# A kernel that plans its own order: new lengths for TensorE's and VectorE's pieces in the plan

## The chip, the cores and the metric

The kernel runs on one NeuronCore of a Trainium2 chip, in one launch. The metric is the device time of that launch in microseconds, the median of the runs shown. A core has five engines that matter here, each with its own instruction stream: TensorE (PE, with PEld for its weight loads), VectorE (DVE), ScalarE (ACT), GpSimd (POOL) and SyncE (SP), which only issues DMAs.

## The reference

It is one layer of a hybrid decoder trunk in float32. A prompt of 1024 tokens and 8 single tokens of a sample group share the weights, so that the kernel works on 1032 columns. D is 1024, there are 4 heads of 256 over 256 memory tokens, and the hidden width of the last part is 2816.

```python
def layer(x, pool_hist, conv_hist, start_pos, mk, mv, g_mix, w_in, pool_map_w, pool_map_b, pool_scale,
          conv_dw_w, conv_dw_b, conv_ln_g, conv_ln_b, w_out, g_attn, w_q, w_o, g_ffn, w_gate, w_up, w_down):
    h = rmsnorm(x, g_mix)
    u = h @ w_in
    a = u[..., :POOL_WIDTH]
    val = u[..., POOL_WIDTH:POOL_WIDTH + CONV_CH]
    gate = u[..., POOL_WIDTH + CONV_CH:]
    glu = val * jax.nn.sigmoid(gate)
    a_ext = jnp.concatenate([pool_hist, a], axis=1)
    g_ext = jnp.concatenate([conv_hist, glu], axis=1)
    ya = pool_mixer(a_ext, start_pos, pool_map_w, pool_map_b, pool_scale)
    yb = conv_mixer(g_ext, conv_dw_w, conv_dw_b, conv_ln_g, conv_ln_b)
    x = x + jnp.concatenate([ya, yb], axis=-1) @ w_out
    x = x + cross_attn(rmsnorm(x, g_attn), mk, mv, w_q, w_o)
    h = rmsnorm(x, g_ffn)
    x = x + (jax.nn.silu(h @ w_gate) * (h @ w_up)) @ w_down
    return x, a_ext[:, -POOL_HIST:], g_ext[:, -CONV_HIST:]
```

`pool_mixer` subtracts each channel from its mean over a trailing window of 2, 4, 8 or 16 tokens and applies a 128x128 map to each group. `conv_mixer` is a depthwise convolution of width 31, a layer norm and a swish. `cross_attn` takes keys and values of the memory, which `mem_kv` makes with `w_k` and `w_v` and which are outputs too. A last rmsnorm gives `y`.

## The kernel before

Activations lie with channels on the 128 partitions and tokens along the free axis. Float32 products are made of three passes of a rounded type: every operand is split into a high half (a rounded copy) and a low half (what the copy lost), and `PASSES` multiplies high by high, high by low and low by high. So each weight tile and each activation tile needs two pieces of work before TensorE may read it: the high half on ACT or POOL (`split`, L346 or L348), the low half on DVE or POOL (L357). For some weights the low half is an accumulating DMA from POOL's queue instead (`split_by_dma`, L368 to L375).

The stages follow each other: input projection with convolution and pooling (matmuls of 344 columns, L457); keys and values of the memory (L827, 256 columns, and L901, 512 columns); the pool map `pmap` and the two output projections `oa` and `ob`; queries, scores and values of the attention; its output projection `po`; then the gated feed-forward part. That part is written as a block product with seven instead of eight multiplications a 2x2 block (`product`, L1290, 258 columns a matmul): VectorE adds each product's bank into its sums (`plus_sums`, L1305), ScalarE copies some of them (`copy_sums`, L1309), and either VectorE or GpSimd does the products and sums between SBUF tiles (L1331, L1313). The up and gate half runs over 22 tiles f, the down half over 16 units u of four chunks, and a last plain part (`fd`, L1587) over what is left of the hidden width.

PSUM holds two wide buffers (`mm`) and two of one bank (`ms`). Every third `product` takes the two `ms` banks, `pr_0` and `pr_1`, and the others an `mm` buffer. A new product can only start in a buffer when its last reader is through.

What sets the order: the kernel body does not issue instructions. It records pieces with `add`: which engines may do the piece, and for each a length in microseconds, the function that emits it, and what it reads and writes. `Program.order` then plays the pieces against each other as a list scheduler. It holds a time at which each engine is free, starts at each step the piece that can start first (within a slack of 0.02 to 0.3 us the one recorded earlier), gives a piece that several engines may do to the one that ends it first, assigns buffers, and keeps VectorE's pieces with two SBUF inputs (`lock=True`) out of GpSimd's. The instructions are issued in that order on each engine. So a length in the plan costs nothing on the chip, but moves pieces in an engine's queue and from one engine to another.

In the plan a VectorE piece is a fixed part and 1.05 ns a column. The fixed part is 0.065 us up to the attention's output projection and 0.148 from there on:

```python
    fixed = {"DVE": 0.065}
    def dve(n):
        return fixed["DVE"] + 0.00105 * n
```

A TensorE piece has a number written out at each place: 0.146 a matmul of 344 columns, 0.109 of 256, 0.217 of 512, 0.1195 of 258 in `product`, 0.1097 of 258 in the last part.

## Time and profile before

| | |
|---|---|
| median of 3 runs | 1264.19 us (1262.49 to 1268.23) |
| the profiled execution's own time | 1266.04 us |
| its span | 1264.2 us |
| PE, DVE, ACT, POOL busy, share of the span | 96%, 72%, 42%, 39% |
| granted TensorE clock, mean | 0.991 |

The page of the profile gives busy time by engine, the span in 40 slices with the granted clock of TensorE, and groups of instructions. Further views are asked of the trace: who waited for whom, the instructions in order of time (start, duration, engine, line, operation, the idle time before it and what ended that), and the busy time of each engine in chosen stretches. A matmul row's duration is its time in the pipeline, so the rate of matmuls is read from a stretch and its count.

### The profile page before, as it was taken

How to read it: one execution, taken by the hardware profiler on the slowest of the kernel's cores; microseconds unless marked ns; L12 is line 12 of the kernel's file. 1: busy time of each engine (PE TensorE's matmuls, PEld its weight loads, DVE VectorE, ACT ScalarE, POOL GpSimd, SP SyncE). 2: the span in 40 equal slices, each digit the busy share in tenths (PEclk: the TensorE clock that was granted, in tenths of full speed). 3: DMA queues.
4: the chain of work that ended last, by engine and by line, in shares of the span. 5: the costliest groups of instructions: out<-in, count | busy, mean ns of one | idle time of the engine just before them, and what ended most of it. 6: DMA issues, size and time to landing. Idle time of an engine off the chain costs nothing.

```text
span 1264.2 us, 22138 instructions
## 1 busy us (share of the span) xinstructions
PE 1218.6 (96%) x8958; PEld 1196.0 (95%) x8958; DVE 909.9 (72%) x1542; ACT 531.8 (42%) x733; POOL 497.8 (39%) x436
## 2 busy tenths in 40 slices
PE   8999997999999999999999999999999999999996
PEld 7999986999999889989999999999999989999996
DVE  7899888667367786578776868686766767766644
ACT  6766658454233443453222222222222355533544
POOL 3578741032101112125353334334433558768401
PEclk9999997999999999999999999999999999999998
DMA  7447696644265663231333133313313598889703
GB/s 278 104 83 167 144 248 171 204 106 158 89 220 198 233 259 143 85 118 59 110 101 108 61 119 109 109 60 109 118 68 118 207 297 231 215 209 246 173 23 113
DMA packets 60453, 188.62 MB, mean 149 GB/s; under 512 B 8064, under 2 KB 11840, under 8 KB 59072
## 3 DMA queue, kind: packets, MB, share of 16 engines
q1 hardware_dynamic: 52288, 157.74, 35.3%
q0 software_dynamic: 8064, 29.47, 13.1%
q8 instruction: 70, 1.15, 0.4%
q14 instruction: 31, 0.25, 0.1%
HBM read 153.55 MB, written 33.64 MB: 148 GB/s over the span
## 4 chain that ended last, share of the span: by engine, by line
PE 73%; DVE 8%; issue 7%; DMA 6%; ACT 3%; POOL 2%; SPq 0%; DVEq 0%; POOLq 0%; ACTq 0%
PE pr L1290 41%; PE ps L457 12%; PE fd L1587 5%; PE oa L457 4%; PE ob L457 4%; DVE cacc L663 2%; DMA dr<-in_w_dn 2%; PE sc L1000 2%; PE pv L1058 2%; DMA raw<-in_w_v 2%; DVE su L1331 1%; DMA hb<-hb 1%; POOL w L357 1%; ACT hb L368 1%; PE psg L457 1%
## 5 line engine op out<-in xcount | busy, mean ns | idle before, releaser
L1305 DVE TENSOR_TENSOR su<-pr,su 128x258 f32<-128x258 f32 (+1 forms) x204 | 109.5, 558 | 98.2 <-PE pr L1290 91.6
L1290 PE MATMUL pr<-ab,wG 128*128 128x258 f32 x1056 | 134.8, 284 | 6.1 <-DVE su L1305 3.8
L1290 PEld LDWEIGHTS pr<-ab,wG 128*128 128x128 f32 x1056 | 129.9, 189 | 7.8 <-DVE su L1305 4.4
L1290 PE MATMUL pr<-ab,wTa 128*128 128x258 f32 x1056 | 134.1, 283 | 0.0
L1290 PE MATMUL pr<-ab,wTb 128*128 128x258 f32 x1056 | 130.5, 283 | 0.0
L1290 PEld LDWEIGHTS pr<-ab,wTa 128*128 128x128 f32 x1056 | 130.0, 189 | 0.0
L1290 PEld LDWEIGHTS pr<-ab,wTb 128*128 128x128 f32 x1056 | 128.5, 189 | 0.0
L457 PE MATMUL ps<-xop,w 128*128 128x344 f32 x720 | 114.1, 320 | 0.6 <-DMA w<-in_w_in 0.6
L457 PEld LDWEIGHTS ps<-xop,w 128*128 128x128 f32 x720 | 113.3, 188 | 0.9 <-DMA w<-in_w_in 0.9
L1290 PE MATMUL pr<-hb,dV 128*128 128x258 f32 x768 | 99.5, 286 | 3.1 <-ACT x L1309 2.1
L1290 PEld LDWEIGHTS pr<-hb,dV 128*128 128x128 f32 x768 | 96.0, 192 | 3.9 <-ACT x L1309 2.4
L457 PE MATMUL ps<-xq,w 128*128 128x344 f32 x576 | 94.8, 321 | 0.0
L457 PE MATMUL po<-oo,w 128*128 128x344 f32 x576 | 91.0, 320 | 0.4 <-DVE oo L1063 0.4
L457 PEld LDWEIGHTS po<-oo,w 128*128 128x128 f32 x576 | 90.7, 188 | 0.7 <-DVE oo L1063 0.7
L457 PEld LDWEIGHTS ps<-xq,w 128*128 128x128 f32 x576 | 90.6, 188 | 0.1
L1305 DVE TENSOR_TENSOR x<-pr,x 128x258 f32<-128x258 f32 (+1 forms) x122 | 63.7, 556 | 28.8 <-PE pr L1290 25.7
L1290 PE MATMUL pr<-hb,dW 128*128 128x258 f32 x576 | 75.6, 284 | 3.9 <-DMA hb<-hb 2.5
L663 DVE SCALAR_TENSOR_TENSOR cacc<-glu,vec,cacc 128x511 f32<-128x511 f32 (+14 forms) x116 | 77.0, 741 | 0.0
L1290 PEld LDWEIGHTS pr<-hb,dW 128*128 128x128 f32 x576 | 71.7, 189 | 5.1 <-DMA hb<-hb 3.2
L1331 DVE TENSOR_TENSOR su<-su,Rf 128x516 f32<-128x516 f32 x66 | 64.6, 981 | 10.8 <-ACT su L1338 10.4
L1587 PE MATMUL fd<-ho,w 128*128 128x258 f32 x576 | 70.0, 283 | 0.0
L1587 PEld LDWEIGHTS fd<-ho,w 128*128 128x128 f32 x576 | 69.4, 189 | 0.1
(319 smaller groups left out, 2330.2 us busy)
## 6 DMA issues: line engine op xcount, KB each, us to landing
gr<-in_w_gu SPq DMA_DIRECT2D x44, 512.0 KB, 3.4
hs<-hb SPq DMA_DIRECT2D x28, 516.0 KB, 6.9
hb<-hb POOLq DMA_DIRECT2D x21, 516.0 KB, 9.2
hb<-su SPq DMA_DIRECT2D x8, 1032.0 KB, 4.5
dr<-in_w_dn SPq DMA_DIRECT2D x16, 512.0 KB, 8.8
spcache_k<-in_cache_k SPq DMA_DIRECT2D x12, 512.0 KB, 4.7
raw<-in_w_in SPq DMA_DIRECT2D x10, 512.0 KB, 5.3
w<-in_w_in POOLq DMA_DIRECT2D x9, 512.0 KB, 6.8
```

What stands on the lines that cost most here:

```text
L357: e.tensor_tensor(dst(1), src(), f32(dst(0)), ALU.subtract)
L368: e.activation(dst(p), src, AF.Copy, scale=factor)
L457: e.matmul(ps[:, c, :CW], w[:, wi, cols], x[:, xi, c * CW : (c + 1) * CW], start=first and p == 0, stop=last and p == 2)
L663: e.scalar_tensor_tensor(acc[h][:, n:], src[:, : HALF - n], w, acc[h][:, n:], ALU.mult, ALU.add)
L1000: e.matmul(bank()[:, i * NMEM : (i + 1) * NMEM], qop[2 * h + dt][:, qi, tt * P : (tt + 1) * P], kk[:, ki, 2 * (h % 2) + dt], start=(dt == ...
L1058: e.matmul(ps[:, c], v[:, vi, m, col : col + P], pT[h][m][:, pi, sl], start=(m == 0 and p == 0), stop=(m == 1 and p == 2))
L1290: e.matmul(bank(c), w[:, wi, cols(j)], xs[0](j, xi)[:, c * TQ : (c + 1) * TQ], start=j == 0 and p == 0, stop=j == nj - 1 and p == 2)
L1305: from_sums(sums, "DVE", dve, lambda e, src, sl: e.tensor_tensor(as_banks(o(sl), src), src, as_banks(a(sl), src), ALU.add), [akey], [okey])
L1331: add({"Pool": pool_tt(TH), "DVE": dve(TH)}, lambda e: e.tensor_tensor(o(), o(), b(), ALU.mult), r + [(su[f], q)], [(su[f], q)], lock=True)
L1587: e.matmul(view(i), w[:, wi, col : col + P], hops[k][:, xi, lo + i * width // count : lo + (i + 1) * width // count], start=(k == 0 and p ...
```

## The change

The plan gets one function for TensorE's matmuls, 6 ns and 0.44 ns a column, in place of the numbers written out, and VectorE keeps the fixed part of 0.065 us to the end. By that function a matmul of 344 columns becomes 0.157 (was 0.146), of 256 columns 0.119 (0.109), of 512 columns 0.231 (0.217), of 258 columns in `product` 0.1195 as before and in the last part 0.1195 (0.1097). No instruction is added, removed or resized but for the pieces that go to another engine: counted over the whole order, 113 pieces go from GpSimd to VectorE, 90 from VectorE to GpSimd, 27 from GpSimd to ScalarE and 22 from ScalarE to GpSimd. Lines from 288 to 1512 stand one lower in the new file.

```diff
--- before.py
+++ after.py
@@ -280,13 +280,14 @@
         return ap.rearrange("p (c n) -> p c n", c=NCH)
 
 
+    def pe(n, count=1):
+        return (0.006 + 0.00044 * n) * count
+
     def act(n, ps=False, ptrs=0):
         return (0.05 if ps else 0.093) + 0.000833 * n + 0.093 * ptrs
 
-    fixed = {"DVE": 0.065}
-
     def dve(n):
-        return fixed["DVE"] + 0.00105 * n
+        return 0.065 + 0.00105 * n
 
     def pool_tt(n):
         return 0.09 + 0.00216 * n
@@ -457,7 +458,7 @@
                     e.matmul(ps[:, c, :CW], w[:, wi, cols], x[:, xi, c * CW : (c + 1) * CW],
                              start=first and p == 0, stop=last and p == 2)
 
-        add({"PE": 0.146 * 3 * len(spans)}, emit, list(wkeys) + (keys or [(x, 0), (x, 1)]),
+        add({"PE": pe(CW, 3 * len(spans))}, emit, list(wkeys) + (keys or [(x, 0), (x, 1)]),
             [(ps, c) for c in spans])
 
     def all3(ps):
@@ -826,7 +827,7 @@
                     for p, (wi, xi) in enumerate(PASSES):
                         e.matmul(ps[:, 0, i * NMEM : (i + 1) * NMEM], w[:, wi, block_cols(k)], memg[k // 4][:, xi, k % 4],
                                  start=(k == 0 and p == 0), stop=(k == KT - 1 and p == 2))
-                add({"PE": 0.327}, emit, wkeys + [(memg[k // 4], p, k % 4) for p in range(2)], [(ps,)])
+                add({"PE": pe(NMEM, 3)}, emit, wkeys + [(memg[k // 4], p, k % 4) for p in range(2)], [(ps,)])
         kf = scr(f"kf{q}", (P, 2, NMEM))
         add({"DVE": dve(512)}, lambda e: e.tensor_tensor(
             kf[:], ps[:, 0].rearrange("p (i m) -> p i m", i=2), Rm().unsqueeze(1).to_broadcast([P, 2, NMEM]), ALU.mult),
@@ -900,7 +901,7 @@
                         for m in range(2):
                             e.matmul(ps[:, m], memg[k // 4][:, xi, k % 4, m * P : (m + 1) * P], w[:, wi, col : col + 512],
                                      start=(k == 0 and p == 0), stop=(k == KT - 1 and p == 2))
-                add({"PE": 1.3}, emit, wkeys + [(memg[k // 4], p, k % 4) for p in range(2)], [(ps,)])
+                add({"PE": pe(512, 6)}, emit, wkeys + [(memg[k // 4], p, k % 4) for p in range(2)], [(ps,)])
         vf = scr(f"vf{c}", (P, 2, 512))
         for m in range(2):
             add({"ACT": act(512, True, 1)}, lambda e, m=m: e.activation(
@@ -1001,7 +1002,7 @@
                                  kk[:, ki, 2 * (h % 2) + dt], start=(dt == 0 and p == 0), stop=(dt == 1 and p == 2))
 
         o = 2 * (h % 2)
-        add({"PE": 1.31}, emit, [(qop[2 * h + dt], p) for dt in range(2) for p in range(2)] + [(kk, p, o) for p in range(2)], [pk])
+        add({"PE": pe(NMEM, 12)}, emit, [(qop[2 * h + dt], p) for dt in range(2) for p in range(2)] + [(kk, p, o) for p in range(2)], [pk])
         st = buf(f"sm{h}_{i2}", "sm", (P, 8))
 
         def top(e):
@@ -1058,7 +1059,7 @@
                         e.matmul(ps[:, c], v[:, vi, m, col : col + P], pT[h][m][:, pi, sl],
                                  start=(m == 0 and p == 0), stop=(m == 1 and p == 2))
 
-            add({"PE": 1.3}, emit, [(v, 0), (v, 1)] + [(pT[h][m], p, c) for p in range(2) for m in range(2)], [(ps, c)])
+            add({"PE": pe(512, 6)}, emit, [(v, 0), (v, 1)] + [(pT[h][m], p, c) for p in range(2) for m in range(2)], [(ps, c)])
             add({"ACT": act(512, True)}, lambda e, c=c, sl=sl: e.activation(oo[:, 0, sl], ps[:, c], AF.Copy), [(ps, c)], [(oo, 0, c)])
             add({"DVE": dve(512)}, lambda e, c=c, sl=sl: e.tensor_tensor(oo[:, 1, sl], ps[:, c], f32(oo[:, 0, sl]), ALU.subtract),
                 [(ps, c), (oo, 0, c)], [(oo, 1, c)])
@@ -1292,7 +1293,7 @@
 
         for n in range(0, nj, nj // steps):
             js = range(n, n + nj // steps)
-            add({"PE": 0.1195 * 6 * len(js)}, lambda e, js=js: emit(e, js),
+            add({"PE": pe(TQ, 6 * len(js))}, lambda e, js=js: emit(e, js),
                 [(w, 0), (w, 1)] + [k for j in js for k in xs[1][j]], [k for _, _, k in sums])
         return sums
 
@@ -1509,7 +1510,6 @@
         hops.append(ho)
 
 
-    fixed["DVE"] = 0.148
     for n in O_ORDER:
         proj_o(n)
         j, i = n % 4, n // 4
@@ -1588,7 +1588,7 @@
                                  start=(k == 0 and p == 0), stop=(k == 5 and p == 2))
 
         for w, keys, ks in ((wa, ka, range(4)), (wb, kb, (4, 5))):
-            add({"PE": 0.000425 * 3 * len(ks) * width}, lambda e, ks=ks: emit(e, ks),
+            add({"PE": pe(width // count, 3 * len(ks) * count)}, lambda e, ks=ks: emit(e, ks),
                 keys + [(hops[k], p) for k in ks for p in range(2)], [(ps,)])
         j, i = n // 2, n % 2
         xk = (x2[j], i, c)
```

**ScalarE between the values and the pool map.** `vf` is the copy of a finished `vps` buffer, `dop` the high half of a pooled group, `yf` the copy of a finished `pmap` buffer, `w` a high half or the negated copy of a weight. Before, the eleven rows up to the first `yf`:

```order
L346 ACTIVATE dop1_1861<-win1_1795 128x1032
L368 ACTIVATE w29_1873<-raw29_1845 128x1024
L368 ACTIVATE w29_1873<-w29_1873 128x1024
L906 ACTIVATE vf0_1892<-vps0_1803,rmc_77 128x512 x2
L346 ACTIVATE vv0_1909<-vf0_1892 128x1024
L643 ACTIVATE cp_593<-y2_1082,csum_75 128x504
L346 ACTIVATE dop0_1935<-win0_1884 128x1032
L346 ACTIVATE w27_1947<-raw27_1774 128x1024
L368 ACTIVATE w28_1968<-raw28_1832 128x1024
L368 ACTIVATE w28_1968<-w28_1968 128x1024
L848 ACTIVATE yf3_1976<-pmap3_1958,pb_s_76,vec_68 128x1032
```

The eleven rows up to the first `yf` in the new order:

```order
L347 ACTIVATE w26_1848<-raw26_1799 128x512
L907 ACTIVATE vf0_1892<-vps0_1802,rmc_77 128x512 x2
L347 ACTIVATE vv0_1911<-vf0_1892 128x1024
L347 ACTIVATE dop0_1922<-win0_1875 128x1032
L347 ACTIVATE w27_1954<-raw27_1826 128x1024
L369 ACTIVATE w28_1956<-raw28_1839 128x1024
L369 ACTIVATE w28_1956<-w28_1956 128x1024
L347 ACTIVATE kT1_1969<-kf2_1965 128x512
L369 ACTIVATE w29_1977<-raw29_1962 128x1024
L369 ACTIVATE w29_1977<-w29_1977 128x1024
L849 ACTIVATE yf3_2003<-pmap3_1979,pb_s_76,vec_68 128x1032
```

`dop1` no longer stands before `vf0` (GpSimd makes it now), the two copies of `w29` moved from before `vf0` to just ahead of `yf3`, and `kT1` went ahead of `yf3` too.

**VectorE at the end of an up and gate tile f.** `pr32_0` and `pr32_1` are the two `ms` banks of a product, which are read a second time here; `su4` are the sums of tile 4. Before:

```order
L1305 TENSOR_TENSOR su4_6232<-pr33_6332,su4_6232 128x516
L1305 TENSOR_TENSOR su4_6232<-pr32_0_6299,su4_6232 128x258
L1331 TENSOR_TENSOR su4_6232<-su4_6232,Rf_5333 128x516
L1305 TENSOR_TENSOR su4_6232<-pr32_1_6300,su4_6232 128x258
L1305 TENSOR_TENSOR su4_6232<-pr34_6364,su4_6232 128x516
L357 TENSOR_TENSOR wU5_6397<-gr5_1_6102,wU5_6397 128x512
L1331 TENSOR_TENSOR su4_6232<-su4_6232,Rf_5333 128x516
```

Now:

```order
L1306 TENSOR_TENSOR su4_6233<-pr33_6332,su4_6233 128x516
L1306 TENSOR_TENSOR su4_6233<-pr32_0_6302,su4_6233 128x258
L1306 TENSOR_TENSOR su4_6233<-pr32_1_6303,su4_6233 128x258
L358 TENSOR_TENSOR wTa6_6390<-ta6_6361,wTa6_6390 128x1024
L358 TENSOR_TENSOR wU5_6423<-gr5_1_6103,wU5_6423 128x512
L1332 TENSOR_TENSOR su4_6233<-su4_6233,Rf_5339 128x516
L1306 TENSOR_TENSOR su4_6233<-pr34_6364,su4_6233 128x516
```

The product with `Rf` (L1331) between the two banks is gone to GpSimd, and the two banks are read one behind the other; the low half of `wTa6` (L358) follows. Before, six tiles f had the product between the two reads; now none has.

**VectorE at the first unit of the down half.** `x` and `pp` are the sums of the down half, `dt` differences of raw weights, `dW` and `dV` low halves of its weights. Before, from the last sum of the up half:

```order
L1305 TENSOR_TENSOR su21_10016<-pr153_10172,su21_10016 128x516
L1305 TENSOR_TENSOR x2_0_10057<-pr154_10208,x2_0_10057 128x516
L1305 TENSOR_TENSOR x2_0_10057<-pr155_0_10232,x2_0_10057 128x258
L1305 TENSOR_TENSOR x2_0_10057<-pr155_1_10233,x2_0_10057 128x258
L1331 TENSOR_TENSOR su21_10016<-su21_10016 128x516 x2
L1431 TENSOR_TENSOR dt1_10286<-dr1_9956 128x256 x2
L1431 TENSOR_TENSOR dt1_10286<-dt1_10286,dr1_9956 128x256
L357 TENSOR_TENSOR dW1_10226<-dr1_9956,dW1_10226 128x512
L1305 TENSOR_TENSOR x2_0_10057<-pr156_10249,x2_0_10057 128x516
L1305 TENSOR_TENSOR pp0_10087<-pr158_0_10288,pp0_10087 128x258
L1305 TENSOR_TENSOR x2_0_10057<-pr159_10308,x2_0_10057 128x516
L1305 TENSOR_TENSOR pp0_10087<-pr158_1_10289,pp0_10087 128x258
```

Now:

```order
L1306 TENSOR_TENSOR su21_10016<-pr153_10173,su21_10016 128x516
L1306 TENSOR_TENSOR x2_0_10057<-pr154_10210,x2_0_10057 128x516
L1332 TENSOR_TENSOR su21_10016<-su21_10016,Rf_5339 128x516
L1332 TENSOR_TENSOR su21_10016<-su21_10016 128x516 x2
L1432 TENSOR_TENSOR dt1_10104<-dt1_10104,dr1_9954 128x256
L1432 TENSOR_TENSOR dt1_10104<-dr1_9954 128x256
L1432 TENSOR_TENSOR dt1_10104<-dr1_9954,dt1_10104 128x256
L358 TENSOR_TENSOR dW1_10226<-dr1_9954,dW1_10226 128x512
L1306 TENSOR_TENSOR x2_0_10057<-pr155_0_10234,x2_0_10057 128x258
L1306 TENSOR_TENSOR x2_0_10057<-pr156_10251,x2_0_10057 128x516
L1306 TENSOR_TENSOR x2_0_10057<-pr155_1_10235,x2_0_10057 128x258
L358 TENSOR_TENSOR dV1_10292<-dt1_10104,dV1_10292 128x1024
```

The reads of the banks `pr155_0` and `pr155_1` come behind three products of the up half, three differences and `dW`, and the low half of `dV1` is VectorE's (it was GpSimd's).

## The prediction

> **What bounds the kernel now.** I read the page first: busy time by engine, and the granted clock in 40 slices.
>
> ```profile
> PE 1218.6 (96%) x8958; PEld 1196.0 (95%) x8958; DVE 909.9 (72%) x1542; ACT 531.8 (42%) x733; POOL 497.8 (39%) x436
> PEclk9999997999999999999999999999999999999998
> ```
>
> TensorE is the bound, and its matmuls don't change. What an order can win or lose is time in which TensorE stands still (1264.2 − 1218.6 = 45.6 us) or runs at a lower clock. Next, by stage, busy time in stretches (start and end, length, then PE, PEld, DVE, ACT and POOL busy with instructions, clock, DMA):
>
> ```profile
> 0.00:148.00 148.00, 140.00 (x864) 137.18 (x865) 129.44 (x191) 101.61 (x132) 93.83 (x116) 1.00 0.56 149
> 148.00:232.00 84.00, 73.40 (x422) 67.68 (x421) 71.90 (x98) 50.32 (x59) 27.23 (x23) 0.92 0.81 227
> 232.00:555.00 323.00, 319.01 (x2041) 310.55 (x2040) 215.86 (x511) 133.79 (x206) 47.56 (x48) 1.00 0.47 161
> 555.00:1004.00 449.00, 442.92 (x3662) 440.69 (x3662) 329.92 (x457) 123.57 (x169) 188.74 (x118) 1.00 0.29 100
> 1004.00:1156.00 152.00, 145.03 (x1174) 143.05 (x1173) 103.00 (x184) 75.40 (x91) 108.83 (x103) 0.99 0.90 252
> 1156.00:1264.20 108.20, 98.29 (x806) 96.89 (x804) 59.78 (x105) 47.13 (x77) 31.56 (x30) 0.97 0.44 113
> ```
>
> TensorE stands still for 10.6 us between 148 and 232 (keys, values, pool map), 6.1 in the up and gate tiles, 7.0 in the down half. The 8.0 of the first stretch and the 9.9 of the last are mostly the loads ahead of the first matmul and the norm after the last, which keep their order. TensorE's waits name the releasers (us in total, times, longest):
>
> ```profile
> PE pmap L457 <- ACT yf L848: 5.0, 1, 5.0
> PE pr L1290 <- DVE su L1305: 4.7, 4, 1.3
> PE oa L457 <- ACT yf L848: 3.0, 1, 3.0
> ```
>
> **The plan against the trace.** Is the new plan nearer to the chip? Rates from long rows of TensorE and the spacing of VectorE's rows:
>
> ```profile
> 161.36 22.27 PE L901 MATMUL vps<-w,memg 128*128 128x512 f32 x96
> 267.81 45.20 PE ob L457 x288
> 663.06 118.47 PE pr L1290 x983
> 779.79 0.69 DVE L1249 TENSOR_TENSOR ta<-gr 128x512 f32<-128x512 f32 x1
> 780.39 0.69 DVE L1249 TENSOR_TENSOR ta<-tb,gr 128x512 f32<-128x512 f32 x1
> L1305 DVE TENSOR_TENSOR su<-pr,su 128x516 f32<-128x516 f32 x104 | 71.7, 691 | 71.0 <-PE pr L1290 66.8 <-ACT su L1309 2.2 <-issue 1.3
> ```
>
> 512 columns take 22.27 / 96 = 0.232 us, 344 columns 45.20 / 288 = 0.157, 258 columns 118.47 / 983 = 0.1205. The new function gives 0.231, 0.157 and 0.1195; the old numbers 0.217, 0.146 and 0.1195. For VectorE both fixed parts are in the trace: one piece alone takes 0.691 = 0.148 + 516 x 0.00105, but two of 512 columns in a row start 0.60 apart, which is 0.065 + 512 x 0.00105 = 0.603. So 0.148 is the length of a piece and 0.065 what it occupies. I take it that the plan gets truer of TensorE in the first half and of VectorE's load in the second, while a piece that something waits for is now planned 0.08 us too short there.
>
> **The change, place by place.** All is made against the profiled execution's 1266.0 us.
>
> *One late weight.* Before, GpSimd worked 2.43 us on a gate first and only then issued the load that adds up a weight's low half:
>
> ```profile
> 107.07 2.43 POOL L695 TENSOR_TENSOR t<-t,Rx 128x1032 f32<-128x1032 f32 x1 [0.74 <-ACT t L694]
> 109.44 0.88 POOL L375 DMA_DIRECT2D w<-in_w_in  x1
> 116.75 1.52 PE L457 MATMUL ps<-xop,w 128*128 128x344 f32 x8 [0.63 <-DMA w<-in_w_in]
> ```
>
> In the new order this load stands ahead of that piece, so it is 2 us earlier and the 0.63 goes: −0.6 (bounds −0.6 and 0).
>
> *Values to pool map, 148 to 232.* These rows (start, duration, in brackets the wait) tell the story:
>
> ```profile
> 188.28 1.07 ACT L346 ACTIVATE dop<-win 128x1032 fp32r<-128x1032 f32 x1 [6.85 <-DVE win L804]
> 192.31 1.25 ACT L906 ACTIVATE vf<-vps,rmc 128x512 f32<-128x512 f32 x2
> 199.10 1.20 ACT L848 ACTIVATE yf<-pmap,pb_s,vec 128x1032 f32<-128x1032 f32 x1
> 199.44 0.68 DVE L831 TENSOR_TENSOR kf<-kps,side 128x512 f32<-128x512 f32 x1
> 200.35 5.53 PE L457 MATMUL pmap<-dop,w 128*128 128x344 f32 x18 [5.05 <-ACT yf L848]
> 205.68 3.35 PE L827 MATMUL kps<-memg,w 128*128 128x256 f32 x24
> 216.46 14.61 PE L457 MATMUL oa<-opa,w 128*128 128x344 f32 x81 [3.02 <-ACT yf L848]
> 199.60:206.50 6.90, 6.15 (x22) 6.15 (x23) 4.78 (x6) 5.04 (x6) 2.85 (x3) 0.51 0.68 176
> 216.70:220.10 3.40, 3.40 (x13) 3.40 (x13) 3.26 (x6) 3.40 (x6) 0.00 (x0) 0.50 0.98 218
> L357 DVE TENSOR_TENSOR w<-raw,w 128x1024 fp32r<-128x1024 f32 x15 | 18.4, 1225 | 9.4 <-ACT w L346 9.4
> ```
>
> ScalarE stood 6.85 us in front of `dop1`; so `vf0`, whose matmuls ended at 161.36 + 22.27 = 183.6, came only at 192.31, and the next two `pmap` waited for `yf3` and `kf2`. In the new order `dop1` is GpSimd's, and between `kf1` and `kf2` VectorE has two low halves of weights less (2 x 1.225) and some 2 us of pieces that now come later. I put `kf2` 4 us earlier, at 195.4, ready at 196.1. But ScalarE then does `kT1` and two copies of `w29` ahead of `yf3`, 0.6 + 2 x 1.06 by the rows' rate of 1.07 for 1032 columns. `yf3` ends at 196.1 + 0.6 + 2.1 + 1.2 = 200.0, only 0.3 earlier than the 200.3 of before, while one `pmap` goes ahead of it from 196.1. The other follows at 200.0 and ends at 201.4; `opa3`, `dop2` and `yf1` (1.05 + 1.06 + 1.2) let the next `kps` start at 203.3, 2.4 before the 205.68 of now. Its 48 matmuls run in one piece (48 x 0.12 = 5.8, to 209.1), then `pmap2` to 210.5. The first `oa` needs `kf3` off VectorE, which has 15.1 us of rows between `kf2` and it (counted in the order, at each row's median; 11.7 before): 196.1 + 15.1 + 0.7 = 211.9. Before it was 216.46: −4.5. After that, twelve mean subtractions stand ahead of the sum that frees the first `oa` buffer: 8 x 0.6 us, four small ones and the sum of 1.2, against 36 x 0.157 = 5.65 us of matmuls, about 1.1 of new waiting. Half clock cost (6.15 + 3.40) / 2 = 4.8 us in the two rows; most of the first is inside the 4.5, and I leave one window of 3.40 (1.7). So −4.5 + 1.1 = −3.4, and the last window stays as it is. Bounds: −9 if `oa` starts behind `pmap2` and no half clock is left, +3 if `kf2` is not earlier and `kf3` has its 15.1 − 11.7 = 3.4 more. I take −3.4.
>
> [...]
>
> *Up and gate tiles.* One of three equal stops:
>
> ```profile
> 782.41 2.40 POOL L357 TENSOR_TENSOR wTa<-ta,wTa 128x1024 fp32r<-128x1024 f32 x1
> 782.62 2.74 DVE L1331 TENSOR_TENSOR su<-su,Rf 128x516 f32<-128x516 f32 x1
> 785.28 1.02 DVE L1305 TENSOR_TENSOR su<-pr,su 128x258 f32<-128x258 f32 x2
> 785.76 2.43 PE L1290 MATMUL pr<-ab,wG 128*128 128x258 f32 x18 [1.26 <-DVE su L1305]
> 786.82 0.68 DVE L1331 TENSOR_TENSOR su<-su,Rf 128x516 f32<-128x516 f32 x1
> ```
>
> The product with `Rf` takes 0.68 alone and 2.74 beside GpSimd's low half; it stands between the reads of the two banks, so the second bank is free 1.26 us late. The waits by releaser say 4.7 in four times; this one and its two like are 3.8. Now the banks are read in a row, before that product: 1.16 + 0.34 us after the start of `wU`'s product, well inside its 24 x 0.12 = 2.9. So −3.8. That GpSimd's new product meets VectorE's low half of `wTa` costs VectorE up to 2.7 us ahead of the next sum; that sum's buffer is wanted two products of 2.9 us later, so it is covered. Bounds −3.8 and 0 (as much again lost elsewhere, VectorE having some 23 us more in this half by the order and the median rows).
>
> *Down half.* At its first unit VectorE reads `pr155` and `pr156` behind one more product with `Rf`. Products are 12 matmuls, 1.45 us, and a buffer is wanted again two to three products later; in the new order about 5 us of rows (0.7 + 0.7 + 1.2 + 1.2 + 0.6 + 0.7) lie ahead against 4.3 of cover: +1 (0 to +2.9, if the product is stretched as above). The loads of raw weights stop TensorE later:
>
> ```profile
> 1036.46 0.94 ACT L346 ACTIVATE dW<-dr 128x512 fp32r<-128x512 f32 x2 [5.70 <-DMA dr<-in_w_dn]
> 1037.93 1.86 PE L1290 MATMUL pr<-hb,dV 128*128 128x258 f32 x12 [2.15 <-ACT x L1309]
> L357 POOL TENSOR_TENSOR dV<-dt,dV 128x1024 fp32r<-128x1024 f32 x13 | 31.5, 2427 | 7.0 <-ACT dV L346 6.3
> L357 DVE TENSOR_TENSOR dV<-dt,dV x3: 1224/1224/1226, 1075.8 to 1130.5; 128x1024 fp32r<-128x1024 f32 x3
> ```
>
> ScalarE waits for `dr`, with a sum's copy queued behind. `dr3` waits for the raw buffer that `dV1`'s low half frees; VectorE makes that in 1.224 instead of GpSimd's 2.427, and earlier. But the DMA engines are 90% busy in this stretch, so I count half of the stop with its half-clock window of 1.7: −(2.15 + 1.7) / 2 = −1.9 (−3.9 to 0).
>
> Attention and `po` are reordered within a unit or two, and I count 0 (−2 to +2).
>
> Sum: −0.6 − 3.4 − 3.8 + 1.0 − 1.9 = −8.7, so 1266.0 − 8.7 = 1257.3 for a profiled execution. The median shown lies 1.85 under the profiled one: 1255.5.
>
> **Rivals.** *Only the tiles gain.* The new queue ahead of `yf3` and `kf3` takes back what the earlier `kf2` gives, and the DMAs set the down half. For it: ScalarE's 3.3 us of new work ahead of `yf3`, the 90% DMA. Against: three causes of the old stop are gone. −0.6 − 3.8 + 1.0 = −3.4: 1260.8.
>
> *VectorE late in the down half, slower.* Seven low halves of `dV` are VectorE's instead of three, in one queue with the sums of 1.45 us products. From 1.224 alone plus 2.427 blocked by GpSimd, 3.65 us, it decides when that exceeds the 2.9 us of two products: 0.8, and a sum of 0.7 behind it. Over 12 of 16 units that is +18; with −0.6 − 3.4 − 3.8 the time is 1264.2 + 10.2 = 1274.4. For it: VectorE's queue is the tighter there. Against: its 103 us of 152, and GpSimd's differences taken over in exchange.
> [...]
>
> *The whole stop goes.* At the low bounds of the stage and the loads: −0.6 − 9 − 3.8 + 1 − 3.9 = −16.3: 1248.
>
> **How the numbers follow.** Chances: the forecast 0.50 (own range 1251 to 1260), only the tiles 0.27, slower 0.15, the whole stop 0.08. About 0.5% (6.3 us, below 1257.9 or above 1270.5) is what a measurement of this kernel tells from no change. Faster: 0.38 of the first, 0.02 of the second, the last, 0.48. Slower: 0.12 of the third. The rest, 0.40, within. The range is 1247 to 1269: what is left out is most of the slower case and the edge of the fastest.
>
> **What would show it.** Right: no wait of `wG` for `su` near 661, 784 and 907; `oa` from about 212 instead of 216.5; `yf3` still some 200. Wrong: a wait of `oa` or `pmap` as long as now, or half-clock windows as many; VectorE's `dV` rows ahead of sums that TensorE waits for; new waits for `su` of a microsecond, repeated in each tile.

## The result, and the profile after

The changed kernel takes 1284.99 us (median; 1280.66 to 1286.68) against 1264.85 us of the kernel before: a ratio of 1.0153, 95% interval 1.0131 to 1.0175. It is slower by about 20 us. The forecast was 1255.5 us, with a range from 1247 to 1269: sign and size were wrong. The profiled execution took 1286.68 us, span 1284.9, against 1266.04 and 1264.2.

Where the time went is read by cutting both spans at the same matmuls: the first one, the first of the values (`vps`), of the mixer's output (`oa`), of the scores (`sc`), of the output projection (`po`), of the tiles (`wG`), of the down half (`dW`) and of the last projection (`fd`). Stretches of the kernel before (start and end, length, then busy time of PE, PEld, DVE, ACT and POOL with instructions, clock, DMA share, GB/s):

```profile
161.36:216.46 55.10, 44.50 (x231) 39.30 (x229) 47.44 (x65) 36.16 (x41) 15.49 (x15) 0.91 0.75 208
340.62:464.65 124.03, 120.04 (x782) 113.39 (x781) 90.84 (x323) 50.35 (x114) 10.88 (x23) 1.00 0.62 220
556.43:1010.48 454.05, 447.88 (x3702) 445.72 (x3703) 333.05 (x462) 124.98 (x170) 191.48 (x120) 1.00 0.30 104
1010.48:1182.26 171.78, 165.71 (x1345) 163.91 (x1345) 118.48 (x212) 83.91 (x101) 127.03 (x118) 0.99 0.88 236
```

The same four stretches of the changed kernel:

```profile
163.19:220.73 57.54, 46.57 (x230) 40.12 (x229) 48.00 (x72) 33.85 (x38) 23.71 (x17) 0.88 0.82 218
345.30:473.02 127.72, 121.37 (x782) 113.08 (x781) 93.89 (x331) 50.00 (x115) 9.29 (x19) 1.00 0.62 214
564.87:1014.20 449.33, 448.24 (x3703) 446.27 (x3704) 345.40 (x481) 128.02 (x172) 156.06 (x99) 1.00 0.30 104
1014.20:1202.71 188.51, 171.20 (x1346) 168.88 (x1345) 129.13 (x221) 82.78 (x100) 121.38 (x114) 0.95 0.81 219
```

| stretch | before | after | change | forecast |
|---|---|---|---|---|
| first matmul to values | 156.4 | 158.4 | +2.0 | −0.6 |
| values to `oa` | 55.1 | 57.5 | +2.4 | −3.4 |
| `oa` to scores | 124.2 | 124.6 | +0.4 | 0 |
| attention (scores to `po`) | 124.0 | 127.7 | +3.7 | 0 |
| `po` to tiles | 91.8 | 91.9 | +0.1 | 0 |
| up and gate tiles | 454.1 | 449.3 | −4.7 | −3.8 |
| down half | 171.8 | 188.5 | +16.7 | −0.9 |
| last projection to the end | 82.0 | 82.2 | +0.2 | 0 |

The tiles gain what was forecast. The down half loses four fifths of the whole: TensorE stands still there for 17.3 us (6.1 before), and behind its waits the granted clock is 0.50 for 13.9 us (3.4 before), an estimated 5 us more, half of the difference. The first two rows are hard to tell from scatter one by one: in seven profiles with the old order up to `oa` (some are runs of the next section) they take 155.7 to 158.1 and 54.6 to 55.5 us, in six with the new order 156.0 to 160.4 and 54.4 to 57.5. Together they are 210.8 to 213.6 with the old and 213.2 to 216.5 with the new order, some 3 us more. Of TensorE's waits in the changed kernel from the values on (total, times, longest):

```profile
PE pr L1291 <- DVE x L1306: 11.7, 6, 4.3
PE pr L1291 <- DMA hb<-hb: 5.1, 3, 2.4
PE vps L902 <- DMA w<-in_w_v: 4.4, 1, 4.4
PE kps L828 <- DMA w<-in_w_k: 2.7, 1, 2.7
PE pmap L458 <- ACT yf L849: 1.1, 1, 1.1
PE oa L458 <- ACT yf L849: 1.0, 1, 1.0
```

The 5.0 of `pmap` and the 3.0 of `oa` for `yf` are nearly gone, as the forecast had it, but 4.4 for the low half of a value weight has come ahead of them, and 2.7 for that of a key weight (1.9 before). The three stops of `wG` for `su` are gone. Six stops for a sum `x`, VectorE's in the down half, take 11.7 us; before, four such stops took a ninth of that:

```profile
PE pr L1290 <- DVE x L1305: 1.3, 4, 0.8
```

One of the six stops, from the rows of VectorE, SyncE and TensorE in order of time (start, duration, in brackets the wait):

```profile
1065.84 0.34 SPq L337 DMA_DIRECT2D dr<-in_w_dn  x1
1069.68 0.70 DVE L1306 TENSOR_TENSOR pp<-pr,pp 128x516 f32<-128x516 f32 x1 [0.83 <-PE pr L1291]
1076.29 0.43 DVE L1432 TENSOR_TENSOR dt<-dr 128x256 f32<-128x256 f32 x1 [5.92 <-DMA dr<-in_w_dn]
1076.63 0.69 DVE L1306 TENSOR_TENSOR x<-pr,x 128x516 f32<-128x516 f32 x1
1077.37 2.95 PE L1291 MATMUL pr<-hb,dV 128*128 128x258 f32 x12 [2.65 <-DVE x L1306]
```

VectorE isn't busy here. It stands for 5.92 us in front of the first difference `dt` of the next unit's weight, because that raw weight hasn't landed; the sum that would free TensorE's buffer stands behind in the same queue. Fifty us later the same happens again, 8.52 us long, with a stop of 2.00:

```profile
1112.59 0.41 SPq L337 DMA_DIRECT2D dr<-in_w_dn  x1
1127.22 0.43 DVE L1432 TENSOR_TENSOR dt<-dr 128x256 f32<-128x256 f32 x1 [8.52 <-DMA dr<-in_w_dn]
1127.56 2.56 DVE L1306 TENSOR_TENSOR x<-pr,x 128x516 f32<-128x516 f32 x5
1128.30 1.70 PE L1291 MATMUL pr<-hb,dW 128*128 128x258 f32 x12 [2.00 <-DVE x L1306]
```

The load was issued at 1112.59 and used at 1127.22, 14.6 us later. By its constants the planner reckons 0.45 + 0.65 + 0.52 MB / 0.36 MB per us + 0.95 = 3.5 us when no other planned transfer is ahead. The planner is plain Python and can be played again without the chip: for these two loads, used 10.5 and 14.6 us after their issue, it plans 5.7 and 6.3 us. In its plan TensorE stands still for 2.5 us in the whole down half (2.0 in the plan of before), so the 16.7 us are no part of the plan.

### The profile page after: what moved, and what is told of

Read it like the earlier page. It is cut to its first block, busy times and chain, and to the rows that moved or that the text cites. A ratio compares the mean times of both kernels' runs of the same rounds, so it can differ in the third digit from the quotient of the medians.

```text
span 1284.9 us, 22121 instructions
## 1 busy us (share of the span) xinstructions
PE 1228.4 (96%) x8958; PEld 1202.0 (94%) x8958; DVE 928.8 (72%) x1570; ACT 535.2 (42%) x738; POOL 468.6 (36%) x403
## 4 chain that ended last, share of the span: by engine, by line
PE 66%; DVE 14%; DMA 9%; issue 4%; ACT 3%; POOL 3%; SPq 0%; DVEq 0%; ACTq 0%; POOLq 0%
PE pr L1291 37%; PE po L458 7%; PE fd L1587 5%; PE ps L458 5%; DVE cacc L664 4%; PE ob L458 3%; PE oa L458 3%; DMA dr<-in_w_dn 2%; DMA hs<-hb 1%; PE pv L1059 1%; DVE spcache_k L1098 1%; DMA spcache_k<-in_cache_k 1%; DMA hb<-hb 1%; PE kps L828 1%; PE sc L1001 1%
## 5 line engine op out<-in xcount | busy, mean ns | idle before, releaser
L1291 PE MATMUL pr<-ab,wTb 128*128 128x258 f32 x1056 | 130.5, 283 | 0.1
L1291 PEld LDWEIGHTS pr<-ab,wTb 128*128 128x128 f32 x1056 | 128.3, 189 | 0.4 <-DVE su L1306 0.4
L1291 PE MATMUL pr<-hb,dV 128*128 128x258 f32 x768 | 102.4, 290 | 8.0 <-DVE x L1306 8.0
L1291 PE MATMUL pr<-hb,dW 128*128 128x258 f32 x576 | 78.4, 290 | 9.3 <-DMA hb<-hb 5.1
L1291 PEld LDWEIGHTS pr<-hb,dW 128*128 128x128 f32 x576 | 74.4, 196 | 10.5 <-DMA hb<-hb 5.7
L1306 DVE TENSOR_TENSOR x<-pr,x 128x516 f32<-128x516 f32 (+1 forms) x122 | 62.8, 555 | 22.3 <-PE pr L1291 20.9
L358 POOL TENSOR_TENSOR w<-raw,w 128x1024 fp32r<-128x1024 f32 (+1 forms) x19 | 42.5, 2244 | 91.0 <-ACT w L347 86.2
L1332 DVE TENSOR_TENSOR su<-su,Rf 128x516 f32<-128x516 f32 x70 | 59.2, 848 | 14.7 <-ACT su L1339 13.9
```

What stands on the lines that cost most here:

```text
L358: e.tensor_tensor(dst(1), src(), f32(dst(0)), ALU.subtract)
L1291: e.matmul(bank(c), w[:, wi, cols(j)], xs[0](j, xi)[:, c * TQ : (c + 1) * TQ], start=j == 0 and p == 0, stop=j == nj - 1 and p == 2)
L1306: from_sums(sums, "DVE", dve, lambda e, src, sl: e.tensor_tensor(as_banks(o(sl), src), src, as_banks(a(sl), src), ALU.add), [akey], [okey])
L1332: add({"Pool": pool_tt(TH), "DVE": dve(TH)}, lambda e: e.tensor_tensor(o(), o(), b(), ALU.mult), r + [(su[f], q)], [(su[f], q)], lock=True)
```

## Experiments

Each is compared with the kernel before on the same chip, and a ratio is to that; stretches are those of the table, each from the profile of its run.

**The two edits apart, and where VectorE's loses.** First TensorE's lengths alone (a diff against the changed kernel):

```diff
+    fixed = {"DVE": 0.065}
     def dve(n):
-        return 0.065 + 0.00105 * n
+        return fixed["DVE"] + 0.00105 * n
...
+    fixed["DVE"] = 0.148
     for n in O_ORDER:
```

> TensorE's new lengths alone; VectorE's fixed part is 0.148 from the output projection on, as before. Theory A (the two edits act in different stretches and add): the start of the feed-forward comes 8.4 us later than before, as in the changed kernel, the up and gate tiles keep their three stops and the down half its old 172 us from its first product to the last projection's first; about 1273 us. Theory B (the order of the down half tips with anything that shifts it): the down half loses 10 us or more here too; 1283 or above.

VectorE's fixed part alone (against the kernel before):

```diff
-    fixed["DVE"] = 0.148
     for n in O_ORDER:
```

> VectorE's 0.065 throughout alone, TensorE's old numbers. Theory A: all is as before up to the output projection, the tiles gain 4.7 us and the down half loses 16.7; about 1277 us. Theory B: the down half's loss depends on where it starts, which is 8.4 us earlier here, so that anything from 1260 (no loss) up can come.

The switch back to 0.148 only at the down half, with the new lengths and then with the old ones:

```diff
     later(lambda: down_blocks(0, DOWN_ORDER[4:]))
+    fixed["DVE"] = 0.148
     units = 4 * CHUNKS
```

> The changed kernel, but VectorE's fixed part is 0.148 from the first unit of the down half on (0.065 up to there). Theory A: the tiles gain 4.7 us and the down half is as before, so only the first half's 8.4 us are lost: about 1268.5 us. Theory B: the down half loses 10 us or more whatever its numbers: 1279 or above.

> The kernel before, with VectorE's fixed part 0.065 through the up and gate tiles as well, and 0.148 only from the first unit of the down half on. Theory A: only the tiles' gain is left, 4.7 us: about 1260 us, faster than both kernels. Theory B: the down half loses 10 us or more: 1270 or above.

| run | time, ratio (95%) | start to tiles | tiles | down half |
|---|---|---|---|---|
| before | 1265.81 | 556.4 | 454.1 | 171.8 |
| lengths alone | 1271.41, 1.0037 (1.0012 to 1.0063) | 563.0 | 453.2 | 173.4 |
| fixed part alone | 1277.04, 1.0078 (1.0053 to 1.0103) | 557.2 | 448.3 | 188.4 |
| both, 0.148 from the down half | 1274.94, 1.0058 (1.0033 to 1.0083) | 563.2 | 449.9 | 180.5 |
| old lengths, 0.148 from the down half | 1264.95, 0.9993 (0.9978 to 1.0008) | 556.2 | 448.3 | 176.5 |

The edits act in different stretches, as theory A says: the lengths cost 6.6 us up to the tiles, the fixed part gains 5.7 in them and loses 16.6 after them. But putting 0.148 back at the down half doesn't bring the 171.8 back: with the new lengths 8.7 us of the loss are left, and with the old ones the last run, which should have kept the tiles' gain, is no faster than the kernel before. There theory A is wrong. (The 176.5 of that run by itself says little: the next part shows one order at 171.5 to 176.5.)

**The late raw weight.** Two ways to take VectorE out of that wait, both on the changed kernel. In the first, two of the four differences can't be VectorE's; in the second, all may, and only the plan's idea of the load's arrival is moved.

```diff
-            add({"Pool": pool_tt(256), "DVE": dve(256)}, lambda e: e.tensor_tensor(s(q)(), a(), b(), op), keys, [(t, q)], lock=True)
+            either = {"Pool": pool_tt(256)} if q in (0, 3) else {"Pool": pool_tt(256), "DVE": dve(256)}
+            add(either, lambda e: e.tensor_tensor(s(q)(), a(), b(), op), keys, [(t, q)], lock=True)
```

> The changed kernel, but of the four differences of each down weight the two that read the raw weight alone can only go to GpSimd; VectorE keeps the two that follow them. Theory C (in the changed kernel VectorE stands in front of such a difference until the raw weight lands, 5.9 and 8.5 us, with sums of products queued behind): its waits for the raw weight end, the two stops of TensorE of 2.65 and 2.00 us and their half clock go, and the down half (first product to the last projection's first) falls from 188.5 to about 180 us, the time to about 1277. Theory D (VectorE has simply too much work there): a dozen pieces of 0.41 us less change little, 186 us or more, about 1283. Rival: GpSimd becomes the late one, with 190 us or more.

```diff
-        dma(lambda: dn_raw[u][:], lambda: io["w_dn"][u], 4 * P * D, w=[(dn_raw[u],)])
+        dma(lambda: dn_raw[u][:], lambda: io["w_dn"][u], 4 * P * D, w=[(dn_raw[u],)], late=4.0)
...
-                end = free["DMA"] + self.DMA_LATENCY
+                end = free["DMA"] + self.DMA_LATENCY + t.late
```

> The changed kernel, but the plan takes a raw down weight to land 4 us later than it reckons now; each piece may go to the same engines as before. Theory C: VectorE's differences stand later in its queue, its waits for the raw weight shrink by about 4 us, the stops of 2.65 and 2.00 go and the down half falls from 188.5 to about 180 us; about 1277. Theory D: VectorE's work is the same, so the down half stays within 3 us of 188.5; about 1284.

VectorE's waits in the down half of the changed kernel, then of the second run:

```profile
DVE dt L1432 <- DMA dr<-in_w_dn: 14.4, 2, 8.5
DVE dt L1432 <- POOL dV L358: 3.7, 3, 2.5
```

```profile
DVE dt L1432 <- DMA dr<-in_w_dn: 0.6, 1, 0.6
DVE dt L1432 <- POOL dW L358: 0.5, 1, 0.5
```

And the down half of the first and of the second:

```profile
1011.01:1188.77 177.76, 169.00 (x1346) 167.11 (x1345) 125.66 (x208) 83.99 (x100) 117.64 (x123) 0.97 0.85 224
```

```profile
1012.45:1190.05 177.60, 167.01 (x1346) 165.41 (x1345) 125.55 (x218) 81.86 (x98) 124.66 (x117) 0.98 0.85 232
```

Both go from 188.5 to 177.7 us, the times to 1272.62 (1.0048, 1.0026 to 1.0070) and 1273.96 (1.0052, 1.0032 to 1.0073). In the second, VectorE does 218 instructions there instead of 221 and is 125.55 us busy for 129.13: hardly less work, and the wait of 14.4 is 0.6. So most of the 16.7 us is the order against the load, not VectorE's work. How much, scatter blurs: from the first `dW` on, the kernel before and the runs with the keys' and values' lengths alone, the projections' alone and the attention's alone (below) have the same rows in the same order, and take 171.8, 171.5, 175.5 and 176.5 us. The granted clock is 0.99 in the 171.8 us of before and 0.97 in the 176.5 of the attention's lengths. The order of the changed kernel takes 188.5 here and 185.2 and 188.8 in two runs below, so the cures are worth 7 to 11 us. The second cure leaves the stop at the entry of the down half as it was (4.08 us for 4.32), which is most of what is still missing.

The same two cures on the kernel before with 0.065 in all tiles but the last:

```diff
         else:
+            fixed["DVE"] = 0.148
             later(lambda: dn_load(0), "load")
```

> The kernel before with VectorE's fixed part 0.065 through all up and gate tiles but the last, and 0.148 from the last on (its down weights' first piece among them). Theory G (the 5 to 9 us that the down half lost with 0.148 from its first unit on came from the pieces planned short in the last tile): the down half returns to 172 to 174 us, the tiles keep 5 of their 5.8: about 1260. If not: the down half stays at 176 or more and the time at 1265.

> The run with 0.065 up to the last tile and 0.148 from it on, and the two differences that read a raw down weight alone for GpSimd only. Theory C: the 7.3 us that VectorE still stood there for a raw weight, and TensorE's stop of 2.9 behind it, go: the down half falls from 174.9 to about 171 us and the time to about 1260, faster than before by 0.4 percent. If GpSimd's queue becomes the late one: 175 us or more, 1265.

> The run with 0.065 up to the last tile and 0.148 from it on, and a plan that takes a raw down weight to land 4 us later. Theory C: the same stop of 2.9 goes, by order alone: the down half about 171 us, the time about 1260. If the later loads only move the wait to another piece: 175 us or more, 1265.

They took 1264.50 (0.9977, 0.9960 to 0.9995), 1265.34 (0.9994, 0.9983 to 1.0005) and 1262.92 us (0.9967, 0.9953 to 0.9981), with the down half at 174.9, 172.4 and 175.7. The waits for the raw weight went in the last two, but 1260 wasn't reached: in the second the last projection became 2.7 us longer, in the third TensorE's stops came elsewhere. All three down halves lie within the 171.5 to 176.5 of one order, so they don't decide theory G. Tiles and down half together are 625.8 us before (623.9 to 627.2 in the three profiles with its order there) and 624.8, 624.6, 622.2 and 624.1 in the four versions that keep the old lengths. By the medians 1 to 4 of the 5 us gained in the tiles reach the end; what takes the rest back is not settled.

**Which lengths cost the first half.** Of the five lengths that change there, some alone. All but the attention's own (scores and weighted values back at 1.31 and 1.30), with VectorE's two fixed parts as before:

```diff
-        add({"PE": pe(NMEM, 12)}, emit, [(qop[2 * h + dt], p) for dt in range(2) for p in range(2)] + [(kk, p, o) for p in range(2)], [pk])
+        add({"PE": 1.31}, emit, [(qop[2 * h + dt], p) for dt in range(2) for p in range(2)] + [(kk, p, o) for p in range(2)], [pk])
...
-            add({"PE": pe(512, 6)}, emit, [(v, 0), (v, 1)] + [(pT[h][m], p, c) for p in range(2) for m in range(2)], [(ps, c)])
+            add({"PE": 1.3}, emit, [(v, 0), (v, 1)] + [(pT[h][m], p, c) for p in range(2) for m in range(2)], [(ps, c)])
```

> TensorE's new lengths as in the run with these alone, but scores and weighted values keep their old 1.31 and 1.30; VectorE's fixed part as before. Theory E (the attention's own pieces, 8 and 7 percent longer in the plan, cost the 4.3 us between its first scores and the output projection): that stretch comes back from 128.3 to about 124 us, with 2 us lost ahead of it; about 1269. Theory F (what precedes, the query projections or a shift of the samples' work against it, costs it): the stretch stays above 127 us; about 1271.

The kernel before with the attention's own two alone, with keys and values alone (0.327 and 1.3 replaced), and with the projections' 344 columns alone (0.146 replaced):

> The kernel before with new lengths for scores and weighted values alone (1.424 and 1.388 for 1.31 and 1.30); all else, keys, values and projections, as before. The order ahead of the first scores is that of before, so the stretch from the first scores to the output projection (124.0 us before) stands alone. Theory F (the query projections' new lengths cost the attention, not its own pieces): 124 to 125 us. Theory H (VectorE's queue is so tight at the attention's end, and its old order so placed, that any other order loses): 126 us or more.

> The kernel before with new lengths for keys and values alone (0.356 for 0.327 and 1.388 for 1.30). The attention keeps the order of before and should stay at 124 us. Theory I (the 2 us lost from the first value product to the first out projection, with the 4 us wait for the low half of a value weight, come from the values' own lengths): that stretch takes 57 us again (55.1 before), with a wait of 3 us or more for a weight of the values. Theory J (they come from the projections' lengths ahead of it): 54.5 to 55.5 us, no such wait.

> The kernel before with the new length for the projections' 344 columns alone (0.157 for 0.146). Theory J (this length is what turns the first half's gain into a loss): the stretch from the first value product to the first out projection takes 56 to 58 us with a wait of about 4 us for a low half of a value weight, and the attention (first scores to output projection) about 132 us, as in the run without the attention's own lengths; the start of the feed-forward comes 10 us or more later than before; about 1276. If it needs the keys' and values' lengths beside it: 55 us, no such wait.

| new lengths | time, ratio (95%) | values to `oa` | attention |
|---|---|---|---|
| none (before) | 1266.93 | 55.1 | 124.0 |
| all | 1271.41, 1.0037 (1.0012 to 1.0063) | 57.2 | 128.3 |
| all but the attention's | 1280.63, 1.0108 (1.0074 to 1.0141) | 56.0 | 132.4 |
| the attention's | 1267.51, 1.0012 (0.9994 to 1.0031) | 54.8 | 124.9 |
| keys and values | 1257.89, 0.9931 (0.9903 to 0.9958) | 45.3 | 124.1 |
| projections | 1276.10, 1.0067 (1.0041 to 1.0093) | 52.6 | 134.5 |

Theories E, H and I fall. It isn't the attention's own lengths that cost it (E, H), but the projections', those of the queries among them (F); the own lengths take half of that back. And the length of the keys and values, which was to bring the loss ahead of `oa` (I; J expected 54.5 to 55.5), brings the largest gain of all: a version 0.7% faster than the kernel before, from two of the changed numbers. Of its 9.8 us in this stretch 3.9 are lost again in the next, from `oa` to the scores (128.0 for 124.2). The projections' length alone doesn't lose ahead of `oa` either (52.6 for 55.1; J expected 56 to 58); only both together are at 54 to 57.5. These effects don't add.

What the projections' length does to the attention, from its end in the run without the attention's own lengths:

```profile
467.63 5.86 PE L1061 MATMUL pv<-pT,vv 128*128 128x512 f32 x24 [0.33 <-DVE oo L1066]
472.03 0.41 DVE L1100 SCALAR_TENSOR_TENSOR spcache_v<-spcache_v,sbcache_v 128x256 f32<-128x256 f32 x1
...
477.21 0.42 DVE L1100 SCALAR_TENSOR_TENSOR spcache_v<-spcache_v,sbcache_v 128x256 f32<-128x256 f32 x1
477.56 1.88 DVE L1066 TENSOR_TENSOR oo<-pv,oo 128x512 fp32r<-128x512 f32 x3
478.30 2.09 PE L460 MATMUL po<-oo,w 128*128 128x344 f32 x6 [4.81 <-DVE oo L1066]
```

Sixteen products of the samples, 5.5 us, stand in VectorE's queue ahead of the `oo` that the output projection needs. This stop is no misjudged length: it stands in the plan itself. Played again, the planner of this run ends the last weighted values at 450.33 and starts the output projection at 454.59. At 448.39 it gives VectorE the first of the samples' four pieces, ready at 448.31, and then the other three, although the `oo` is ready from 448.60: of pieces that can start, it takes the one recorded earlier. In the plans, TensorE stands still in the attention for 9.2 us in this run and with the projections' length alone, 2.4 in the changed kernel and 1.1 in the kernel before; the stretch takes 132.4, 134.5, 127.7 and 124.0 us on the chip. In the changed kernel the new waits are smaller ones (0.6 to 0.9 us each), 6.3 us in all against 4.0; that their cause is the same was not tried by itself.

**Why the value weights are late in the changed kernel.** ScalarE stands in front of the high half of the keys there, with the copies of the value weights behind it, and SyncE in front of the store of `kf`, with their raw loads behind it; both until VectorE comes to `kf`, which stands behind eight pieces of the convolution:

```profile
162.29 5.30 DVE L664 SCALAR_TENSOR_TENSOR cacc<-glu,vec,cacc 128x508 f32<-128x508 f32 x8
162.84 4.32 SPq L337 DMA_DIRECT2D raw<-in_w_v  x2
167.51 0.68 DVE L832 TENSOR_TENSOR kf<-kps,side 128x512 f32<-128x512 f32 x1
168.22 0.63 ACT L347 ACTIVATE kT<-kf 128x512 fp32r<-128x512 f32 x1 [5.18 <-DVE kf L832]
168.81 1.06 ACT L369 ACTIVATE w<-raw 128x1024 fp32r<-128x1024 f32 x1
174.61 0.86 POOL L376 DMA_DIRECT2D w<-in_w_v  x1 [2.46 <-DMA raw<-in_w_v]
179.81 13.14 PE L902 MATMUL vps<-w,memg 128*128 128x512 f32 x44 [4.40 <-DMA w<-in_w_v]
```

First ScalarE is freed, then SyncE as well, then the down half's cure is added:

```diff
-        split(lambda p: kT[q // 2][:, p, o : o + 2], lambda p: (kT[q // 2], p, o), lambda: kf[:], 512, [(kf,)])
+        kk, keyk = kT[q // 2], lambda p: (kT[q // 2], p, o)
+        add({"DVE": dve(512)}, lambda e: e.tensor_scalar(kk[:, 0, o : o + 2], kf[:], 1.0, 1.0, ALU.mult, ALU.mult), [(kf,)], [keyk(0)])
+        add({"Pool": pool_tt(512), "DVE": dve(512)}, lambda e: e.tensor_tensor(
+            kk[:, 1, o : o + 2], kf[:], f32(kk[:, 0, o : o + 2]), ALU.subtract), [(kf,), keyk(0)], [keyk(1)], lock=True)
```

> The changed kernel, but the high halves of the keys (kT) are VectorE's, right behind kf, and no longer ScalarE's or GpSimd's. Theory K (ScalarE stands 5.2 us in front of kT until VectorE comes to kf, with the copies of the value weights queued behind it): the wait of 4.4 us of the value products for a weight goes, and the stretch from the first value product to the first out projection falls from 57.5 to about 52; the rest of the program keeps its order; about 1279. Rival L (the DMAs carry the value weights too late whatever ScalarE does): the wait stays above 3 us and the stretch at 56 or more; about 1284.

```diff
-        dma(lambda: io["mem_k"][:, 2 * q : 2 * q + 2], lambda: kf[:], 4 * P * 512, r=[(kf,)])
+        dma(lambda: io["mem_k"][:, 2 * q : 2 * q + 2], lambda: kf[:], 4 * P * 512, r=[(kf,)], hold=5.0)
...
-                t.at[e] = max([0.0] + [x + (same if o == e and not t.nbytes else signal) for o, x in t.ends.items()])
+                t.at[e] = max([0.0] + [x + (same if o == e and not t.nbytes else signal) for o, x in t.ends.items()]) + t.hold
```

> The run with the keys' high halves on VectorE, and the store of kf planned 5 us later, which moves three rows on SyncE (two raw loads of value weights go ahead of the store of kf0, three ahead of that of kf1) and no row on any other engine before the first out projection. Theory M (SyncE, standing in front of the store until VectorE comes to kf, is what holds the raw loads): the loads are issued some 4 us earlier, the 6.1 us wait of the value products for a low half falls to 2 or less and the stretch from the first value product to the first out projection from 58.8 to 53 or 54 us; about 1280. Rival L (the loads land late whoever issues them when): the wait stays above 4 us, the stretch above 56; about 1285.

> The run before this one with the down half's cure as well (differences that read the raw weight alone are GpSimd's only). If the parts add: the down half 178 us as there, the first half as in the run before, the attention still 128; about 1269. If theory M falls: 1274.

The times were 1285.78 (1.0153, 1.0122 to 1.0183), 1289.94 (1.0178, 1.0155 to 1.0201) and 1278.33 us (1.0087, 1.0070 to 1.0104). Theory K falls: with ScalarE free, values to `oa` takes 58.8 us, and ScalarE then waits for the raw load itself. TensorE's wait in that run and in the next:

```profile
PE vps L905 <- DMA w<-in_w_v: 6.1, 1, 6.1
```

```profile
PE pmap L458 <- DVE w L358: 5.4, 1, 5.4
PE vps L905 <- DMA w<-in_w_v: 4.6, 1, 4.6
```

and SyncE's in the second, from 148 to 176 us:

```profile
SPq L337 <- POOL w L358: 5.2, 3, 3.7
```

Theory M falls too: the raw loads are issued 3 us earlier (158.78 for 161.74), the wait is 1.5 shorter, the stretch 59.6. SyncE then stands 5.2 us for low halves that GpSimd still has to make before a raw buffer is free (3.9 in the changed kernel), and a later weight stops `pmap` for 5.4 (3.7 in the run before). Rival L's bounds were met both times, but nothing here shows its cause. Each queue that is freed shows the next one behind it; which of them sets this stretch, or whether VectorE's late `kf` alone does, stays open. The last run has the down half at 177.4 us as in the first cure: that part adds. Its other two stretches, 60.4 and 130.5 us, don't gain, so it misses 1269 and 1274.

**The gains together.** Lengths of keys and values alone, with the later raw down weights, once with 0.065 up to the last tile and once with VectorE's two fixed parts as before:

> New lengths for keys and values alone, VectorE's 0.065 up to the last up and gate tile and 0.148 from it on, and raw down weights reckoned to land 4 us later. If the gains add (9 us ahead of the first out projection, 3 to 4 from the tiles on): about 1254, faster than both kernels. If the tiles' gain is given back in the down half: 1258.

> New lengths for keys and values alone, VectorE's two fixed parts as before, and raw down weights reckoned to land 4 us later. The tiles keep their three stops (452 to 454 us); if the later loads help a plan that waits 1 to 4 us for raw weights, the down half falls from 171.5 to about 169 and the time to about 1255; if they only move the waits, 1258.

1258.95 (0.9934, 0.9912 to 0.9956) and 1263.90 us (0.9971, 0.9955 to 0.9988). The gain ahead of `oa` stays in both (45.7 and 45.4 us for that stretch), and what is added to it brings nothing. No version is shown to be faster than the one with the lengths of the keys and values alone.

## Why the prediction was wrong, step by step

Of the 29.4 us between the forecast and the profiled time, 17.6 lie in the down half, 5.8 between the values and `oa`, 3.7 in the attention and 2.6 ahead of the values. The step that decided it is the one on the down half's loads.

**The plan against the trace** was read rightly: the new lengths are nearer to the chip, and 0.148 is a lone piece, 0.065 what it occupies (a row of 516 columns takes 0.69 us, and the one behind it starts after 0.60, in the first two rows below). The warning at its end, that a piece something waits for is now planned 0.08 us too short, was left without a price.

**Up and gate tiles**, −3.8: right, −4.7 measured, and 448 to 451 us in all thirteen profiles with 0.065 there against 451 to 456 in seven without. Both banks are read in a row, and the product with `Rf`, alone again at 0.69, stands ahead of them:

```profile
782.93 0.69 DVE L1332 TENSOR_TENSOR su<-su,Rf 128x516 f32<-128x516 f32 x1
783.53 0.69 DVE L1306 TENSOR_TENSOR su<-pr,su 128x516 f32<-128x516 f32 x1
786.10 0.76 DVE L1306 TENSOR_TENSOR su<-pr,su 128x258 f32<-128x258 f32 x2 [0.37 <-PE pr L1291]
```

**Down loads**, −1.9 (bounds −3.9 to 0): this step failed, in sign. It followed the one stop that was there, ScalarE's in front of `dr`, and asked whether the new order takes it away. It does. It didn't ask which other queue would now stand in front of a raw weight, and "no loss" was set as the upper bound without a reason that excluded one. The trace of before had the row to ask it of. VectorE already stood there for `dr`, and TensorE didn't stop for it:

```profile
DVE dt L1431 <- DMA dr<-in_w_dn: 5.3, 2, 4.0
```

A raw weight issued at 1023.77 in that trace landed 12.6 us later, too. In the new plan VectorE has the first difference of the first of the two loads shown above, which was GpSimd's before; the one at 1127.22 was VectorE's already. That its pieces, planned 0.083 us shorter, make it look free earlier to the planner is the likely reason, argued and not tried piece by piece. What the runs show is the rest: the plan's 5.7 and 6.3 us for loads that took 10.5 and 14.6, and a price of 7 to 11 us (10.8 against the profile above).

**Down half entry**, +1 (0 to +2.9): the place was right, the size not. The stop is 4.32 us, and the clock behind it is at 0.71:

```profile
1017.91 2.17 DVE L1332 TENSOR_TENSOR su<-su,Rf 128x516 f32<-128x516 f32 x1 [1.39 <-ACT su L1339]
1020.01 1.82 DVE L1332 TENSOR_TENSOR su<-su 128x516 f32<-128x516 f32 x2
1024.43 3.81 PE L1291 MATMUL pr<-hb,dV 128*128 128x258 f32 x16 [4.32 <-DVE x L1306]
1024.50:1032.00 7.50, 7.50 (x46) 7.50 (x47) 6.51 (x9) 5.38 (x6) 3.06 (x5) 0.71 1.02 311
```

The 5 us of rows were counted as if they ran one behind the other; VectorE first waits 1.39 us for `silu`, and the product is stretched to 2.17 (0.69 alone, above). The upper bound had the stretch, but neither the wait nor the clock. The second cure of the down half, which leaves this stop, is still 5.8 us above the 171.8 of before; the term was 1.

**Values to pool map**, −3.4 (−9 to +3): +2.4, inside the bounds. The step that failed is "I put `kf2` 4 us earlier, at 195.4": it came at 203.18, and at 200.5 to 203.9 in the six profiles with this order, since value and key weights ahead of it were late (4.4 and 2.7 us here). The working counted ScalarE's and VectorE's rows between `kf1` and `kf2` and took the weights to be there. Why they are late stays open, since theories K and M fall. The gain that it described is real: with the lengths of keys and values alone `kf2` comes at 190.5, `oa` starts right behind the last `pmap`, the bound of −9, and the stretch is 9.8 us shorter.

**Attention**, 0 (−2 to +2): +3.7, and 127.7 to 130.5 us in all eight profiles with that order against 124.0 to 125.1 in nine with the old one. This term was set without following a single queue there, and the two plans, 2.4 and 1.1 us of standing TensorE in this stretch, already pointed to a small loss.

**One late weight**, −0.6: the first wait went, and the next weight of the same kind came 0.76 us late instead.

**The rivals.** "VectorE late in the down half" had the sign, the place and by luck the price (18; 16.7 measured), but not the mechanism: it counted VectorE's work, seven low halves, and the run that leaves the work nearly as it is and moves only the plan's arrival takes most of the loss away. Its 3.65 us for a low half of `dV` stands in no row: in the changed kernel's down half VectorE's six recorded ones took 1.23 us four times, and 2.81 and 3.09 once each. Its chance, 0.15, was too small because "against: its 103 us of 152" looks at how busy the engine is, and the engine stood still.

## What to carry to other kernels

When a plan fills in-order queues, a truer cost can make a slower kernel: ask for every engine what it stands in front of and what is queued behind it, and price a late arrival by that queue, not by the engine's busy share. Before costing a stop at nothing or less, look for rows in which an engine already waits harmlessly; a new order needs only to put something urgent behind them. Play the planner again first: it shows the stops that it makes itself, as in the attention here, though not those of a length that it has wrong, as in the down half. Change the numbers of a plan one at a time: here two of the changed numbers gain 9 us and the others turn it into a loss.
